# Second feed-forward network: the w3 product of all sixteen row tiles as seven block products, with the weight sums made in place

## The chip, the cores and the metric

One core of one Trainium2 chip runs one launch of the whole layer. The time is device microseconds of one execution. The engines that matter are the tensor engine (PE, with its weight loads as PEld), VectorE (DVE), ScalarE (ACT) and the queue of SyncE (SP), which issues the loads of weights. GpSimd (POOL) does next to nothing here.

## The reference

A layer with a gated feed-forward network before and after a mixer, in float32, for 256 rows of width 2048. The change touches only the second feed-forward network, cut here to what matters:

```python
h = _rms_norm(x, g_ffn2) * (1.0 + sc3) + sh3
x = x + 0.5 * ga3 * (jax.nn.silu(h @ w1_b) * (h @ w3_b)) @ w2_b      # w1_b, w3_b: 2048 x 5632, w2_b: 5632 x 2048
x = _rms_norm(x, g_final)
```

## The kernel before

**Precision.** Every float32 product is made of three passes: an operand is split into a high part (a cast to fp32r on ACT) and a low part (the value less the high part, on DVE), and `mm3` (lines 134 to 139) multiplies high by high, high by low and low by high. The activations `h`, transposed, are the stationary operand, the weights the moving one.

**Units and buffers.** Weights come in units of 4 row tiles of 128 by 512 columns (1 MB, one load, 128 x 2048). Three `raw` buffers receive them (pool `raws`, line 68). A unit is split in two halves of 128 x 1024; each half takes one of six `wh` and one of six `wl` buffers (pool `hl`, line 69). A half's buffer is used again six halves later, when PE has read it. So DVE and ACT run at most three units ahead of PE, and a raw buffer is loaded again when the splitting of the unit in it is done.

**Stages of the second network.** The 5632 columns are 11 chunks of 512, in groups: chunks 0 and 1, 2 to 4, 5 to 7, 8 to 10. For each group an up stretch makes `silu(h @ w1) * (h @ w3)`, and a down stretch (`ffn_down`) multiplies by `w2` and adds to `x`. In chunk 0 both up products are plain, 8 units of 24 matmuls of 512 columns. For chunks 1 to 10 the w1 product is plain (4 units, one per group of four row tiles, kg = 0 to 3). The w3 product is plain for kg = 3 and made of block products for kg = 0 to 2: a 2 x 2 by 2 x 2 block product (two row tiles, two halves of the rows of `h`, two blocks of 256 columns) by seven products in place of eight. `left_sums` makes the four sums of blocks of `h` once, in chunk 0 (their high and low parts are `sh`, `sl`). `seven_products` loads a unit whose blocks lie in the order (0,1), (0,0), (1,1), (1,0) for each of two q, makes four sums of weight blocks into a tile `T` of its own (lines 1242 to 1245), splits three raw blocks (768 columns) and four sums (1024 columns) for each q (lines 1252 and 1253), and runs 42 matmuls of 256 columns. They add up in the accumulator `a3` and two banks `m0`, `m1`, from which `sum_up` makes the w3 product at the end of the chunk.

**Order of the work.** The engines run their own queues in order. The program is written in the order of chunks; a scheduler places each engine's instructions by it and by its own times, keeping some matmuls in program order (`pin`). In a chunk the written order was: w1 unit 0, w3 unit 3, the transposes of the chunk before (`flush`), then three times seven products and a w1 unit, with `sum_up` ahead of the last unit.

## Time and profile before

| | |
|---|---|
| median of 3 runs | 2145.2 us (2145.12 to 2149.35) |
| profiled execution: its time, its span | 2147.01 us, 2145.2 us |
| PE busy, DVE busy, ACT busy | 99%, 76%, 48% of the span |
| granted tensor clock, mean | 0.995 |
| second feed-forward network | from about 1415 us on |

The span is the first to the last recorded instruction. Durations of DVE and ACT rows include the end of an instruction that the next one may overlap, and those of matmuls are modelled, so the prediction works with times from start to start.

### The profile page before, as it was taken

Reading aid. Unit: us, or ns where it says so; the run is one execution under the profiler, and the core shown is the slowest. Engines: PE = TensorE matmul, PEld = TensorE weight load, DVE = VectorE, ACT = ScalarE, POOL = GpSimd, SP = SyncE. Lnnn points to the kernel's source line nnn. Section 1 sums busy time; section 2 is a strip of 40 time slices with the busy share of each in tenths; the row PEclk is TensorE's granted clock in tenths of the full one; section 3 lists DMA queues with packets and bytes.
Section 4 is the critical chain, followed back from the end, with each engine's and each line's share of the span. In section 5 each row is a group of like instructions: output and inputs, shape, how many; then the busy total and the mean of one; then the engine's idle time right before and its main releaser. Section 6 shows DMA issues by size and latency. Waiting matters only on the chain.

```text
span 2145.2 us, 26028 instructions
## 1 busy us (share of the span) xinstructions
PE 2113.4 (99%) x10192; PEld 1759.2 (82%) x10192; DVE 1627.6 (76%) x1840; ACT 1036.7 (48%) x1290; POOL 41.7 (2%) x63
## 2 busy tenths in 40 slices
PE   8899999999999999999999999999999999999998
PEld 6677888888888879888877888878888888888886
DVE  6888767788778777565777788887788678857875
ACT  6434443334344465655544434475455445535553
POOL 0000000000000001010000000000000000000000
PEclk9999999999999999999999999999999999999999
DMA  9998768899899855445788788855555645655563
GB/s 368 347 361 322 246 222 322 329 351 346 335 327 334 323 174 188 167 172 199 287 286 306 285 328 312 339 209 188 206 194 189 208 176 196 215 196 195 178 216 118
DMA packets 78670, 550.30 MB, mean 257 GB/s; under 512 B 9361, under 2 KB 9921, under 8 KB 13266
## 3 DMA queue, kind: packets, MB, share of 16 engines
q1 hardware_dynamic: 75744, 542.06, 69.2%
q0 software_dynamic: 1344, 3.17, 0.5%
q10 hardware_dynamic: 1458, 3.40, 0.4%
q8 instruction: 80, 1.31, 0.2%
q14 instruction: 44, 0.36, 0.0%
HBM read 546.47 MB, written 2.12 MB: 256 GB/s over the span
## 4 chain that ended last, share of the span: by engine, by line
PE 90%; DVE 3%; DMA 3%; ACT 2%; issue 1%; POOL 0%; SPq 0%; POOLq 0%; ACTq 0%
PE a L135 9%; PE a L138 9%; PE a L139 9%; PE y L135 9%; PE y L139 9%; PE y L138 9%; DMA raw<-in_w_open 3%; PE pacc L138 2%; PE pacc L139 2%; PE pacc L135 2%; DVE wl L124 2%; PE qkv L135 1%; PE gb L135 1%; PE qkv L138 1%; PE ga L139 1%; PE ga L135 1%
## 5 line engine op out<-in xcount | busy, mean ns | idle before, releaser
L123 ACT CAST wh<-raw 128x1024 fp32r<-128x1024 f32 (+2 forms) x678 | 690.0, 1040 | 890.1 <-DMA raw<-in_w_a 212.9
L124 DVE TENSOR_TENSOR wl<-raw,wh 128x1024 fp32r<-128x1024 f32 (+2 forms) x678 | 804.3, 1208 | 337.1 <-ACT wh L123 335.2
L192 DVE SCALAR_TENSOR_TENSOR raw<-raw,c_bc 128x2048 f32<-128x2048 f32 x144 | 329.2, 2287 | 31.4 <-DMA raw<-in_w_ada 30.1
L135 PE MATMUL a<-wh,hTh 128*128 128x512 f32 (+1 forms) x904 | 340.1, 376 | 0.1
L138 PE MATMUL a<-wl,hTh 128*128 128x512 f32 (+1 forms) x904 | 339.4, 375 | 0.0
L139 PE MATMUL a<-wh,hTl 128*128 128x512 f32 (+1 forms) x904 | 339.2, 375 | 0.0
L135 PE MATMUL y<-wh,gT 128*128 128x512 f32 x704 | 275.7, 392 | 0.2
L138 PE MATMUL y<-wl,gT 128*128 128x512 f32 x704 | 274.1, 389 | 0.0
L139 PE MATMUL y<-wh,gT 128*128 128x512 f32 x704 | 273.7, 389 | 0.0
L139 PEld LDWEIGHTS a<-wh,hTl 128*128 128x128 f32 x904 | 170.2, 188 | 31.2 <-DVE hTl L363 0.3
L135 PEld LDWEIGHTS a<-wh,hTh 128*128 128x128 f32 x904 | 170.3, 188 | 30.3 <-ACT wh L123 0.6
L138 PEld LDWEIGHTS a<-wl,hTh 128*128 128x128 f32 x904 | 170.4, 188 | 29.1
L135 PEld LDWEIGHTS y<-wh,gT 128*128 128x128 f32 x704 | 132.2, 188 | 29.5 <-ACT gT L386 1.8
L139 PEld LDWEIGHTS y<-wh,gT 128*128 128x128 f32 x704 | 132.1, 188 | 27.7 <-DVE gT L387 0.2
L138 PEld LDWEIGHTS y<-wl,gT 128*128 128x128 f32 x704 | 132.2, 188 | 26.9
L138 PE MATMUL pacc<-wl,hTh 128*128 128x512 f32 x360 | 142.9, 397 | 6.7 <-DVE wl L124 6.7
L135 PE MATMUL pacc<-wh,hTh 128*128 128x512 f32 x360 | 138.4, 398 | 6.6 <-ACT wh L123 5.9
L139 PE MATMUL pacc<-wh,hTl 128*128 128x512 f32 x360 | 141.6, 393 | 0.7 <-DVE hTl L545 0.7
L1253 DVE TENSOR_TENSOR wl<-right,wh 128x1024 fp32r<-128x1024 f32 x60 | 73.4, 1224 | 30.6 <-ACT wh L1252 30.0
L1252 ACT CAST wh<-right 128x1024 fp32r<-128x1024 f32 x60 | 63.2, 1053 | 56.4 <-PE m L139 25.2
L138 PEld LDWEIGHTS pacc<-wl,hTh 128*128 128x128 f32 x360 | 68.4, 190 | 25.3 <-DVE wl L124 11.0
L135 PEld LDWEIGHTS pacc<-wh,hTh 128*128 128x128 f32 x360 | 67.8, 189 | 24.3 <-ACT wh L123 9.3
(350 smaller groups left out, 3096.1 us busy)
## 6 DMA issues: line engine op xcount, KB each, us to landing
raw<-in_w_ada SPq DMA_DIRECT2D x144, 1024.0 KB, 6.1
raw<-in_w_b SPq DMA_DIRECT2D x102, 1024.0 KB, 4.8
raw<-in_w_a SPq DMA_DIRECT2D x84, 1024.0 KB, 6.0
raw<-in_w_in SPq DMA_DIRECT2D x60, 1024.0 KB, 5.0
raw<-in_w_open SPq DMA_DIRECT2D x48, 1024.0 KB, 6.9
raw<-in_w_s SPq DMA_DIRECT2D x30, 1024.0 KB, 4.8
raw<-in_w_out SPq DMA_DIRECT2D x16, 1024.0 KB, 6.0
raw<-in_w_proj_a SPq DMA_DIRECT2D x8, 1024.0 KB, 4.8
```

The lines of the kernel that those rows point to most:

```text
L123: last_cast[0] = ACT.copy(wh[:, :w], src)
L124: DVE.tensor_tensor(wl[:, :w], src, wh[:, :w].bitcast(F32), op=ALU.subtract)
L135: m = PE.matmul(out, xh, wh, start=start, stop=False)
L138: PE.matmul(out, xh, wl, start=False, stop=False)
L139: PE.matmul(out, xl, wh, start=False, stop=stop)
L192: last_ada[0] = DVE.scalar_tensor_tensor(out=raw, in0=raw, scalar=1.0, in1=c_bc, op0=ALU.mult, op1=ALU.mult, accum_out=dst)
L1252: ACT.copy(wh[:, :n], src)
L1253: DVE.tensor_tensor(wl[:, :n], src, wh[:, :n].bitcast(F32), op=ALU.subtract)
```

## The change

`seven_products` runs for all four kg, so the plain w3 unit of chunks 1 to 10 goes and a fourth `left_sums` and a fourth unit of reordered weights come. The weight sums are no longer made into a tile of their own but in the raw buffer itself: the three raw blocks of both q are split first, then four sums of 128 x 2 x 256 overwrite the raw blocks, then the four sums of both q are split. The room of `T` goes to the fourth left tile; `left_sums` takes its work tile from the raw buffers. One corner of the accumulator is no longer written, so `sum_up` copies and adds 768 columns of it. In a chunk the written order is now: w1 unit 0, seven products kg = 0, `flush`, w1 unit 1, seven products 1, w1 unit 2, seven products 2, seven products 3, `sum_up`, w1 unit 3.

```diff
         def left_sums(kg):

-            t = f2.tile([P, D], F32, tag="T", name="left")
+            t = raws.tile([P, D], F32, tag="raw", name="left")
             f = t[:, :1024].rearrange("p (t k n) -> p t k n", t=TB, k=4)
             for tb in range(TB):
...
-            sh = f2.tile([P, 4, 2, P], F32R, name=f"sh{kg}")
-            sl = f2.tile([P, 4, 2, P], F32R, name=f"sl{kg}")
+            both = f2.tile([P, 2, 4, 2, P], F32R, tag=f"S{kg}", name=f"S{kg}")
             flat = lambda v: v.rearrange("p s q n -> p (s q n)")
-            ACT.copy(flat(sh), t[:, 1024:])
-            DVE.tensor_tensor(flat(sl), t[:, 1024:], flat(sh).bitcast(F32), op=ALU.subtract)
-            SH.append(sh)
-            SL.append(sl)
+            ACT.copy(flat(both[:, 0]), t[:, 1024:])
+            DVE.tensor_tensor(flat(both[:, 1]), t[:, 1024:], flat(both[:, 0]).bitcast(F32), op=ALU.subtract)
+            SH.append(both[:, 0])
+            SL.append(both[:, 1])

         def seven_products(acc, ms, ap, kg, first, last):
 
             raw = load_unit(ap)
             rv = raw.rearrange("p (q b n) -> p q b n", q=2, b=4)
-            t = f2.tile([P, D], F32, tag="T", name="right")
-            tv = t.rearrange("p (q b n) -> p q b n", q=2, b=4)
-            DVE.tensor_tensor(tv[:, :, 0:2], rv[:, :, 1:3], rv[:, :, 0:1].broadcast_to([P, 2, 2, 256]),
-                              op=ALU.subtract)
-            DVE.tensor_tensor(tv[:, :, 2], tv[:, :, 1], rv[:, :, 1], op=ALU.add)
-            DVE.tensor_tensor(tv[:, :, 3], rv[:, :, 3], tv[:, :, 2], op=ALU.subtract)
+            w = [[], []]
+
+            def split(q, b0, b1):
+                wh = hl.tile([P, 1024], F32R, tag="wh", name="wh")
+                wl = hl.tile([P, 1024], F32R, tag="wl", name="wl")
+                n = (b1 - b0) * 256
+                src = raw[:, q * 1024 + b0 * 256:q * 1024 + b1 * 256]
+                ACT.copy(wh[:, :n], src)
+                DVE.tensor_tensor(wl[:, :n], src, wh[:, :n].bitcast(F32), op=ALU.subtract)
+                w[q].extend((wh[:, i:i + 256], wl[:, i:i + 256]) for i in range(0, n, 256))
+
             for q in range(2):
-                w = []
-                for src in (raw[:, q * 1024 + 256:(q + 1) * 1024], t[:, q * 1024:(q + 1) * 1024]):
-                    n = src.shape[1]
-                    wh = hl.tile([P, 1024], F32R, tag="wh", name="wh")
-                    wl = hl.tile([P, 1024], F32R, tag="wl", name="wl")
-                    ACT.copy(wh[:, :n], src)
-                    DVE.tensor_tensor(wl[:, :n], src, wh[:, :n].bitcast(F32), op=ALU.subtract)
-                    w += [(wh[:, i:i + 256], wl[:, i:i + 256]) for i in range(0, n, 256)]
+                split(q, 1, 4)
+            DVE.tensor_tensor(rv[:, :, 2], rv[:, :, 2], rv[:, :, 0], op=ALU.subtract)
+            DVE.tensor_tensor(rv[:, :, 0], rv[:, :, 1], rv[:, :, 0], op=ALU.subtract)
+            DVE.tensor_tensor(rv[:, :, 1], rv[:, :, 1], rv[:, :, 2], op=ALU.add)
+            DVE.tensor_tensor(rv[:, :, 3], rv[:, :, 3], rv[:, :, 1], op=ALU.subtract)
+            for q in range(2):
+                split(q, 0, 4)
+            for q in range(2):
...
+                v = w[q]
                 for out, x, wt, is_first, is_last in (
-                        (ms[0][:, lo], xs(k, 0), w[0], True, False), (acc[:, 0, lo], xs(k + 1, 0), w[2], False, False),
-                        (acc[:, 0, hi], left(3), w[1], False, True), (ms[1][:, lo], left(0), w[3], True, False),
-                        (acc[:, 1, lo], xs(k + 1, 1), w[6], False, True), (ms[0][:, hi], left(1), w[5], False, True),
-                        (ms[1][:, hi], left(2), w[4], False, True)):
+                        (ms[0][:, lo], xs(k, 0), v[0], True, False), (acc[:, 0, lo], xs(k + 1, 0), v[2], True, False),
+                        (acc[:, 0, hi], left(3), v[1], False, True), (ms[1][:, lo], left(0), v[3], True, False),
+                        (acc[:, 1, lo], xs(k + 1, 1), v[6], True, True), (ms[0][:, hi], left(1), v[4], False, True),
+                        (ms[1][:, hi], left(2), v[5], False, True)):
                     mm3(out, *x, *wt, start=begin and is_first, stop=end and is_last, pin=begin or end)
...
             h = wkB("h3")
-            ACT.copy(h, acc.rearrange("p t n -> p (t n)"))
+            ACT.copy(h[:, :768], acc.rearrange("p t n -> p (t n)")[:, :768])
             r = wkA("r")
             u = r[:, 768:1024]
...
-            DVE.tensor_tensor(u, ms[1][:, 0:256], r[:, 512:768], op=ALU.add)
-            DVE.tensor_tensor(h, h, r, op=ALU.add)
+            DVE.tensor_tensor(h[:, 768:1024], ms[1][:, 0:256], r[:, 512:768], op=ALU.add)
+            DVE.tensor_tensor(h[:, :768], h[:, :768], r[:, :768], op=ALU.add)
...
-                    gemm(a3, up_units(a["w3_b"], c, xs), hook={kg: lambda kg=kg: left_sums(kg) for kg in range(3)})
+                    gemm(a3, up_units(a["w3_b"], c, xs), hook={kg: lambda kg=kg: left_sums(kg) for kg in range(4)})
...
                 a1 = acc_tile("a1")
                 unit(a1, a["w1_b"][0, c], 0, True, False)
                 a3 = acc_tile("a3")
                 ms = [bank("m0"), bank("m1")]
-                unit(a3, a["w3_b"][3, c], 3, True, False)
-                flush()
-                for kg in range(3):
-                    seven_products(a3, ms, a["w3_s"][kg, c - 1], kg, kg == 0, kg == 2)
-                    if kg == 2:
+                for kg in range(4):
+                    seven_products(a3, ms, a["w3_s"][kg, c - 1], kg, kg == 0, kg == 3)
+                    if kg == 3:
                         h3 = sum_up(a3, ms)
-                    unit(a1, a["w1_b"][kg + 1, c], kg + 1, False, kg == 2)
+                    if kg == 0:
+                        flush()
+                    if kg != 2:
+                        unit(a1, a["w1_b"][min(kg, 2) + 1, c], min(kg, 2) + 1, False, kg == 3)
...
-        gfin = f2.tile([P, D], F32, tag="T", name="gfin")
+        gfin = f2.tile([P, D], F32, tag="S0", name="gfin")
         ACT.dma_start(gfin, a["g_final"].to_broadcast([P, D]))
```

How this moves instructions, at three places. In the names, `wh` and `wl` are the high and low part of a half, `raw` a unit's buffer and `right` the tile of weight sums of before; the numbers tell tiles apart.

The first place is VectorE in chunk 2, from the end of the second seven products to the third. Before, where each q had its raw blocks and its sums split in turn, and the sums of the third stood beside the subtractions of the w1 unit ahead of it:

```order
L1253 TENSOR_TENSOR wl_11895<-raw_11859,wh_11894 128x768
L1253 TENSOR_TENSOR wl_11899<-right_11861,wh_11898 128x1024
L1242 TENSOR_TENSOR right_11959<-raw_11957 128x2x512
L1244 TENSOR_TENSOR right_11959<-right_11959,raw_11957 128x2x256
L124 TENSOR_TENSOR wl_11926<-raw_11923,wh_11925 128x1024
L1245 TENSOR_TENSOR right_11959<-raw_11957,right_11959 128x2x256
L124 TENSOR_TENSOR wl_11930<-raw_11923,wh_11929 128x1024
L1253 TENSOR_TENSOR wl_11964<-raw_11957,wh_11963 128x768
L1253 TENSOR_TENSOR wl_11968<-right_11959,wh_11967 128x1024
L1253 TENSOR_TENSOR wl_11993<-raw_11957,wh_11992 128x768
L1253 TENSOR_TENSOR wl_11997<-right_11959,wh_11996 128x1024
```

Now, from the third seven products (raw_11960) to the fourth (raw_12024):

```order
L1254 TENSOR_TENSOR raw_11960<-raw_11960 128x2x256
L1255 TENSOR_TENSOR raw_11960<-raw_11960 128x2x256
L1256 TENSOR_TENSOR raw_11960<-raw_11960 128x2x256
L1257 TENSOR_TENSOR raw_11960<-raw_11960 128x2x256
L1247 TENSOR_TENSOR wl_11975<-raw_11960,wh_11974 128x1024
L1247 TENSOR_TENSOR wl_11979<-raw_11960,wh_11978 128x1024
L1247 TENSOR_TENSOR wl_12027<-raw_12024,wh_12026 128x768
L1247 TENSOR_TENSOR wl_12031<-raw_12024,wh_12030 128x768
L1254 TENSOR_TENSOR raw_12024<-raw_12024 128x2x256
L1255 TENSOR_TENSOR raw_12024<-raw_12024 128x2x256
L1256 TENSOR_TENSOR raw_12024<-raw_12024 128x2x256
L1257 TENSOR_TENSOR raw_12024<-raw_12024 128x2x256
```

The four sums stand together between the splitting of the raw blocks and that of the sums, and no other work lies between them or behind them; the fourth seven products follow the third with no w1 unit between. ScalarE's casts at that place now stand so (L1246 is the cast in `split`):

```order
L1246 CAST wh_11962<-raw_11960 128x768
L1246 CAST wh_11966<-raw_11960 128x768
L1246 CAST wh_11974<-raw_11960 128x1024
L1246 CAST wh_11978<-raw_11960 128x1024
L1246 CAST wh_12026<-raw_12024 128x768
L1246 CAST wh_12030<-raw_12024 128x768
L1246 CAST wh_12038<-raw_12024 128x1024
L1246 CAST wh_12042<-raw_12024 128x1024
```

Before, ScalarE too alternated raw blocks and sums with two casts of a w1 unit between two seven products; now the casts of the sums come after both casts of raw blocks, and eight casts of seven products follow each other.

The second place is PE in the fourth seven products of chunk 2, from the last matmuls with the raw blocks of q = 0 (wh_12026) to those with its sums (wh_12038, wl_12039):

```order
L139 MATMUL a3_11761<-wh_12026,S3_10923 128x256
L135 MATMUL m1_11763<-wh_12038,S3_10923 128x256
L135 MATMUL a3_11761<-wh_12038,hTh_10579 128x256
L135 MATMUL m0_11762<-wh_12038,S3_10923 128x256
L138 MATMUL m1_11763<-wl_12039,S3_10923 128x256
L139 MATMUL m1_11763<-wh_12038,S3_10923 128x256
L138 MATMUL a3_11761<-wl_12039,hTh_10579 128x256
L139 MATMUL a3_11761<-wh_12038,hTl_10580 128x256
L138 MATMUL m0_11762<-wl_12039,S3_10923 128x256
L139 MATMUL m0_11762<-wh_12038,S3_10923 128x256
```

Three matmuls with the high part of the sums were moved ahead of the first with their low part.

The third place is VectorE where chunk 2 ends and chunk 3 begins: the tail of `sum_up`, the first seven products of chunk 3 (raw_12171) and the product with silu (L1324):

```order
L1247 TENSOR_TENSOR wl_12174<-raw_12171,wh_12173 128x768
L1247 TENSOR_TENSOR wl_12178<-raw_12171,wh_12177 128x768
L1254 TENSOR_TENSOR raw_12171<-raw_12171 128x2x256
L1324 TENSOR_TENSOR h3_12088<-h3_12088,silu_12130 128x1024
L1255 TENSOR_TENSOR raw_12171<-raw_12171 128x2x256
L1256 TENSOR_TENSOR raw_12171<-raw_12171 128x2x256
L1257 TENSOR_TENSOR raw_12171<-raw_12171 128x2x256
```

The product with silu, which waits for the end of chunk 2's last w1 unit, stands between the first and the second of the weight sums of chunk 3.

4 lines of the change are left out of this document (2 added, 2 removed).

## The prediction

> **What bounds the kernel now.** I read the page first: engine shares and the chain of work that ended last.
>
> ```profile
> span 2145.2 us, 26028 instructions
> PE 2113.4 (99%) x10192; PEld 1759.2 (82%) x10192; DVE 1627.6 (76%) x1840; ACT 1036.7 (48%) x1290; POOL 41.7 (2%) x63
> PE 90%; DVE 3%; DMA 3%; ACT 2%; issue 1%; POOL 0%; SPq 0%; POOLq 0%; ACTq 0%
> ```
>
> The tensor engine sets the end. But 76% for VectorE is a mean over the whole program; the change lies in the up stretches of the second FFN only, so I looked at one 512-column chunk there (c = 3), by its window, and at its ends in the chain.
>
> ```profile
> 1602.50:1645.75 43.25, 43.25 (x255) 38.47 (x254) 36.48 (x39) 24.75 (x27) 0.00 (x0) 1.00 0.55 195
> 1602.46 0.23 PE a L139
> 1645.72 0.23 PE a L139
> ```
>
> The columns of the first row are the wall time, then busy PE, PEld, DVE, ACT, POOL, then granted clock, DMA share and GB/s. PE is busy throughout at clock 1.00; one chunk takes 1645.72 - 1602.46 = 43.26 us. DVE is busy 36.48 us of it, so it has 6.8 us to spare per chunk. DMA is at 55%. The question is whether what the change takes from PE is worth more than what it puts on DVE's 6.8 us.
>
> **What it saves on PE.** Matmul durations overlap, so I take start-to-start times from PE's rows of chunk c = 2: seven products over one weight tile (42 matmuls of 256 columns), then one plain unit (24 of 512).
>
> ```profile
> 1549.26 0.39 PE L135 MATMUL a<-wh,hTh 128*128 128x512 f32 x1
> 1560.14 0.28 PE L135 MATMUL m<-wh,hTh 128*128 128x256 f32 x1
> 1562.54 0.28 PE L139 MATMUL m<-wh,sl 128*128 128x256 f32 x1
> 1565.17 0.40 PE L135 MATMUL a<-wh,hTh 128*128 128x512 f32 x1
> 1570.64 0.28 PE L135 MATMUL m<-wh,hTh 128*128 128x256 f32 x1
> 1591.64 0.39 PE L135 MATMUL a<-wh,hTh 128*128 128x512 f32 x1
> ```
>
> Seven products: 1565.17 - 1560.14 = 5.03 us, 0.120 per matmul. A unit: 1570.64 - 1565.17 = 5.47 us. Each of the ten chunks c = 1 to 10 swaps one unit for seven products: 0.44 us less, 4.4 us in all. That is the whole gain; 0.2% of the time is 4.3 us, about what a measurement of this kernel can tell from no change. One chunk of PE work becomes 43.26 - 0.44 = 42.82 us; the first of a group has no transposes: it takes 1591.64 - 1549.26 = 42.38 now and 41.94 after.
>
> **What it puts on DVE.** Here are DVE's rows around one block-sum sequence of before.
>
> ```profile
> 1544.11 0.69 DVE L1244 TENSOR_TENSOR right<-right,raw 128x512 f32<-128x512 f32 x1
> 1544.83 0.69 DVE L1245 TENSOR_TENSOR right<-raw,right 128x512 f32<-128x512 f32 x1
> 1592.68 0.95 DVE L1253 TENSOR_TENSOR wl<-raw,wh 128x768 fp32r<-128x768 f32 x1
> 1593.55 1.22 DVE L1316 TENSOR_TENSOR h<-h,silu 128x1024 f32<-128x1024 f32 x1
> 1594.68 0.69 DVE L1245 TENSOR_TENSOR right<-raw,right 128x512 f32<-128x512 f32 x1
> 1653.03 1.23 DVE L1253 TENSOR_TENSOR wl<-right,wh 128x1024 fp32r<-128x1024 f32 x1 [0.43 <-ACT wh L1252]
> 1654.29 1.23 DVE L1242 TENSOR_TENSOR right<-raw 128x1024 f32<-128x1024 f32 x1
> 1655.55 0.69 DVE L1244 TENSOR_TENSOR right<-right,raw 128x512 f32<-128x512 f32 x1
> 1656.16 1.22 DVE L124 TENSOR_TENSOR wl<-raw,wh 128x1024 fp32r<-128x1024 f32 x1
> ```
>
> Start to start, an independent follower comes after 1.14 us (1024 elements, 1593.55 to 1594.68), 0.87 (768, 1592.68 to 1593.55), 0.61 (512, 1655.55 to 1656.16). A follower that must wait for its predecessor comes later: 1.26 (L1253 to L1242, which overwrites what L1253 read), 0.72 (L1244 to L1245). In the changed kernel the four sums stand back to back, each overwrites or reads what the one ahead touched, and the first overwrites what the low-part subtraction ahead of it reads. So each pays the longer spacing. Before, other work stood between.
>
> The round trip to ScalarE comes on top. The casts of the sums can start only when the fourth sum is done, DVE's next instruction is their subtraction, and nothing stands between:
>
> ```profile
> 1561.41 0.84 ACT L1252 CAST wh<-raw 128x768 fp32r<-128x768 f32 x1
> 1562.90 1.05 ACT L1252 CAST wh<-right 128x1024 fp32r<-128x1024 f32 x1 [0.65 <-PE m L139]
> 1565.43 1.05 ACT L1252 CAST wh<-right 128x1024 fp32r<-128x1024 f32 x1 [0.60 <-PE m L139]
> 1566.52 1.22 DVE L1253 TENSOR_TENSOR wl<-right,wh 128x1024 fp32r<-128x1024 f32 x1 [0.44 <-ACT wh L1252]
> 1595.46 1.05 ACT L1252 CAST wh<-right 128x1024 fp32r<-128x1024 f32 x1 [2.59 <-DVE right L1245]
> ```
>
> DVE to ACT costs 0.09 (1594.68 + 0.69 to 1595.46), the cast 1.05, ACT to DVE 0.04 (1566.48 to 1566.52). Call the four halves of a tile p, q (raw blocks, 768) and r, s (sums, 1024). One seven on DVE is now: low part of p 0.87; of q 0.95 + 0.04 until the first sum; three sums at 0.72 and the last 0.69; the round trip 0.09 + 1.05 + 0.04 = 1.18; r and s 2 x 1.14 = 2.28. Sum: 8.17 us, against 5.03 us of matmuls.
>
> The rest of DVE's chunk:
>
> ```profile
> 1648.27 1.28 DVE L387 TENSOR_TENSOR gT<-gT_ps,gT 128x512 fp32r<-128x512 f32 x2
> 1673.73 0.42 DVE L1274 TENSOR_TENSOR r<-m,r 128x256 f32<-128x256 f32 x1
> 1674.25 0.69 DVE L1276 TENSOR_TENSOR r<-m,r 128x512 f32<-128x512 f32 x1
> 1674.86 1.22 DVE L124 TENSOR_TENSOR wl<-raw,wh 128x1024 fp32r<-128x1024 f32 x1
> ```
>
> Four units 4 x 2 x 1.14 = 9.12; the two gT parts 2 x 0.61 = 1.22; the block sums of the output 0.52 (1673.73 to 1674.25) + 0.72 + 0.34 + 0.87 = 2.45 (the 256 without a wait put at 0.34, an estimate from 0.42 less the 0.08 by which the longer ones overlap); the product with silu 1.14. With 4 x 8.17 = 32.68 this is 46.61 us per chunk, against PE's 42.82. DVE becomes the bound: a settled chunk goes from 43.26 to 46.6, plus 0.0 to 0.3 us where DVE waits for a buffer that PE has to free. I take 46.7: 3.4 us more.
>
> **Where PE will stand still.** Six split buffers let DVE and ACT run three units ahead. They hide a late tile when a plain unit follows (5.47 us of PE work for 2.28 us of DVE), but now the third and fourth sevens follow each other. Walk c = 2, the first of a group, from the start of its first unit W0, with the saturated PE: W0 0 to 5.46, S0 to 10.49, W1 to 15.95, S1 to 20.98, W2 to 26.44, S2 to 31.47. The cast of S2's q needs the buffer of S1's q, six halves earlier, which PE frees after S1's matmul 30, at 15.95 + 3.6 + 0.24 = 19.79 (0.24 is what passes from the end of a matmul's 0.12 slot to ACT's start: 1562.54 + 0.12 to 1562.90). Cast 0.84, low part at 20.67, sums from 21.66 to 24.5, cast of r to 25.65, low part of r at 25.69; then s 26.83, S3's p 27.97, q 28.84, its sums 29.83 to 32.68, cast to 33.82, low part of r done at 35.1. PE comes to S3 at 31.47 and can do p (nine matmuls) and, in the planned order, three with r's high parts: it needs the low part at 32.9. It waits 2.25 us. So a first chunk goes from 42.38 to 41.94 + 2.25 = 44.2: 1.8 us more.
>
> What waits behind: S3's end lets the output sums start, W3's end lets silu start, and DVE's product with silu stands in its queue ahead of the next S0's second sum, which is why later chunks settle at DVE's period and not at 44.2.
>
> **Left sums.** A fourth left_sums goes into chunk 0:
>
> ```profile
> 1437.20 1.29 DVE L1219 TENSOR_TENSOR left<-hTh,hTl 128x512 f32<-128x512 f32 x2
> 1438.40 1.23 DVE L124 TENSOR_TENSOR wl<-raw,wh 128x1024 fp32r<-128x1024 f32 x1
> 1439.54 0.42 DVE L1222 SCALAR_TENSOR_TENSOR left<-left 128x256 f32<-128x256 f32 x1
> 1439.87 0.42 DVE L1226 TENSOR_TENSOR left<-left 128x256 f32<-128x256 f32 x1
> raw<-in_w_b SPq DMA_DIRECT2D x102, 1024.0 KB, 4.8
> ```
>
> It costs DVE 1.2 + 4 x 0.34 + 1.14 = 3.7 us. All four now take a turn in the three raw buffers, so the load of w3's third unit starts only when the second left sum has been split, and lands 4.8 us later. By my walk that unit comes 1 to 1.5 us late to PE. Bounds: 0, hidden by the three units ahead, and 8.5, all of 3.7 and a whole landing. I take 1.0, near the lower bound, since PE has 5.47 us per unit and three are ready. The tile for g_final takes S0's place, free before the last down stretch: 0, hidden by that stretch; uncovered, its landing.
>
> **The sum.** Settled chunks 3, 4, 6, 7, 9, 10: 6 x 3.4 = 20.4. First chunks 2, 5, 8: 3 x 1.8 = 5.4. Chunk 1, which begins after chunk 0 but carries gT parts: 3.4, like a settled one. Left sums 1.0. Together 30.2 us. The profiled execution had a span of 2145.2 and took 2147.0, within 0.1% of the median of 2145.2; from the median I get 2175.4, say 2175.
>
> One rule of the Trainium skill speaks for less. VectorE: DVE Perf Modes, section "The DRAIN you can't avoid", reports eight copies that took 13.88 us with a semaphore after each and with one after the last alone, so that a wait on the predecessor costs nothing extra. This trace does not agree: 1.26 against 1.14 and 0.72 against 0.61. By that rule the sum would be the first rival's.
>
> **The rivals.** (1) The waits between the sums cost nothing: 0.87 for q, 0.61 for three sums, so a seven takes 8.17 - 0.12 - 0.33 = 7.72 us and a settled chunk 46.7 - 1.8 = 44.9. Then 6 x 1.6 + 3 x 0.9 (S2 and S3 each save 0.45) + 1.6 + 1.0 = 14.9: 2160. For it: the forms of L1242 and L1244 only resemble the new ones. Against it: both rows above show the longer spacing.
>
> (2) The other side: PE stays the bound. DVE's debt is carried by the six buffers through the chunks and paid back in the down stretches, where DVE has nothing but 2.28 us per 5.47 us unit. The place is S3; it decides where a seven costs DVE no more than (42.82 - 13.93) / 4 = 7.2 us (13.93 is the chunk's other work), that is where about 1 us of the round trip is filled. Then the 4.4 us are gained: 2141. For it: 6.8 us of spare time in DVE's window. Against it: DVE's queue is in order and holds no other work behind the fourth sum.
>
> (3) The raw ring binds: left sums and tiles held longer make loads late, 8.5 us instead of 1.0 in chunk 0: 2183. For it: the in-place tile is freed only after s. Against it: a tile's next load has two other units (over 10 us) before it is wanted, against 4.8.
>
> **How the numbers follow.** Forecast 0.62, rival 1 0.18, rival 2 0.09, rival 3 0.11. Rival 2 in full is faster by about 0.2%, so I split it: faster 0.07, same 0.04 with half-covered cases; slower 0.89. The forecast's own range is 2166 to 2184: 0.2 us per seven either way, 8 us over forty. For 8 in 10 the range reaches below rival 1 and above rival 3: 2153 to 2187; rival 2 stays out.
>
> **What would show it.** Right: chunk-to-chunk distance of 46 to 47 us; DVE busy over 90% in such a window; PE waiting in the fourth seven for wl, over 2 us each; the four sums 0.72 apart; DVE's idle time before r's low part about 1.1 us, named ACT wh. Wrong: a distance of 42.8 and no PE wait (rival 2), sums 0.61 apart and 45 us (rival 1), PE or ACT waiting on DMA for raw (rival 3).

## The result and the profile after

| | before | after |
|---|---|---|
| median of 4 runs each | 2146.9 us (2145.1 to 2149.4) | 2179.7 us (2176.2 to 2184.2) |
| ratio after / before | | 1.0158, 95% interval 1.0140 to 1.0176 |
| profiled execution: time, span | 2147.0, 2145.2 us | 2177.5, 2175.7 us |
| settled chunk (c = 3, 4, 6, 7, 9, 10) | 43.25 to 43.26 us | 47.5 to 48.0 us |

The change makes the kernel 32.7 us slower. The page of after, span, engine shares and chain of waits:

```profile
span 2175.7 us, 26495 instructions
PE 2127.4 (98%) x10372; PEld 1778.1 (82%) x10372; DVE 1677.2 (77%) x1937; ACT 1037.3 (48%) x1311; POOL 41.6 (2%) x63
PE 76%; DVE 15%; ACT 4%; DMA 3%; issue 2%; POOL 0%; SPq 0%; ACTq 0%; POOLq 0%; DVEq 0%
```

The shares of busy time hardly move; the chain does. VectorE's part of it goes from 3% to 15%, 12% of the span, and TensorE's from 90% to 76%. A busy share says how much an engine works, the chain who is waited for.

Where the time went shows in stretches cut at the start of silu (line 1315 before, 1323 after), one silu per chunk. Of after, the first chunk of a group with the down stretch ahead of it (c = 2), then the two settled chunks c = 3 and 4, by windows (wall time, busy PE, PEld, DVE, ACT, POOL, granted clock, DMA share, GB/s):

```profile
1505.70:1594.00 88.30, 87.60 (x468) 75.11 (x467) 68.86 (x71) 41.89 (x49) 3.26 (x6) 1.00 0.56 195
1594.00:1641.75 47.75, 45.33 (x273) 40.75 (x272) 42.24 (x49) 24.73 (x30) 0.00 (x0) 0.96 0.50 186
1641.75:1689.78 48.03, 45.32 (x273) 40.78 (x272) 41.03 (x46) 25.14 (x29) 0.00 (x0) 0.96 0.49 167
```

The first two of the same stretches of before (the third takes 43.25):

```profile
1504.19:1591.84 87.65, 87.65 (x451) 74.59 (x450) 65.28 (x63) 42.06 (x47) 4.41 (x8) 1.00 0.58 204
1591.84:1635.10 43.26, 43.26 (x255) 38.47 (x254) 36.48 (x39) 24.75 (x27) 0.00 (x0) 1.00 0.56 195
```

Over the program: the six settled chunks 26.7 us longer together (4.45 each); the first chunks of the three groups 0.65, 0.85 and 0.77, together 2.3; chunks 0 and 1, from the transposes that feed chunk 0 to the silu of chunk 1, 91.15 in place of 85.69, so 5.5; after the last silu 76.04 in place of 76.07. That is 34.4 us. In this execution everything ahead of chunk 0 happened to end 3.95 us earlier (those transposes start at 1414.55 in place of 1418.50), so the spans differ by 30.5. This opening moves by that much between executions of the same code, as a run below with the same opening shows, and is no part of the change.

VectorE's rows in c = 3 of after, from r's low part of the third seven to the next chunk's product with silu:

```profile
1621.43 4.10 DVE L1247 TENSOR_TENSOR wl<-raw,wh 128x1024 fp32r<-128x1024 f32 x4 [1.17 <-ACT wh L1246]
1625.57 0.69 DVE L1254 TENSOR_TENSOR raw<-raw 128x512 f32<-128x512 f32 x1
1626.29 0.69 DVE L1255 TENSOR_TENSOR raw<-raw 128x512 f32<-128x512 f32 x1
1627.02 0.69 DVE L1256 TENSOR_TENSOR raw<-raw 128x512 f32<-128x512 f32 x1
1627.74 0.69 DVE L1257 TENSOR_TENSOR raw<-raw 128x512 f32<-128x512 f32 x1
1629.62 2.36 DVE L1247 TENSOR_TENSOR wl<-raw,wh 128x1024 fp32r<-128x1024 f32 x2 [1.19 <-ACT wh L1246]
...
1642.81 1.22 DVE L1324 TENSOR_TENSOR h<-h,silu 128x1024 f32<-128x1024 f32 x1 [1.13 <-ACT silu L1323]
```

From r's low part to r's low part of the next seven it is 1629.62 - 1621.43 = 8.19 us, with no other work between. The sums start 0.72 to 0.73 apart, and VectorE stands idle for 1.17 to 1.19 us until ScalarE has cast the sums. The wait in the last row is new in this chunk: VectorE also stands idle for 1.13 us until silu is done. The reason stands in PE's rows of the same seven, the fourth:

```profile
1627.60 0.28 PE L139 MATMUL a<-wh,S 128*128 128x256 f32 x1
1629.64 0.39 PE L135 MATMUL m<-wh,S 128*128 128x256 f32 x1 [1.76 <-ACT wh L1246]
...
1629.98 0.28 PE L135 MATMUL m<-wh,S 128*128 128x256 f32 x1
1630.90 0.39 PE L138 MATMUL m<-wl,S 128*128 128x256 f32 x1 [0.64 <-DVE wl L1247]
...
1634.20 0.41 PE L138 MATMUL a<-wl,S 128*128 128x256 f32 x1
1634.41 0.41 PE L139 MATMUL a<-wh,S 128*128 128x256 f32 x1
```

After p's nine products PE loses 1.92 us to the cast of r (2.04 from start to start, less 0.12 for the product), and 0.80 us to r's low part. From then on the products start 0.21 us apart and not 0.12. The granted clock (the column behind the busy times) in windows of 2 us says why:

```profile
1629.00:1631.00 2.00, 0.72 (x4) 0.52 (x4) 1.38 (x2) 2.00 (x3) 0.00 (x0) 1.00 0.00 0
1631.00:1633.00 2.00, 2.00 (x11) 2.00 (x12) 2.00 (x2) 2.00 (x3) 0.00 (x0) 0.57 0.11 16
1633.00:1635.00 2.00, 2.00 (x12) 2.00 (x12) 2.00 (x3) 1.33 (x2) 0.00 (x0) 0.58 0.78 274
1635.00:1637.00 2.00, 2.00 (x15) 1.84 (x14) 1.85 (x3) 1.29 (x3) 0.00 (x0) 1.00 1.03 434
```

Behind the stall the tensor clock falls to 0.57 for about 3.5 us. Seventeen products at 0.21 in place of 0.12 are about 1.5 us, and these put back the last w1 unit, silu, and VectorE's product with silu, which stands in its queue ahead of the next sums. The clock falls so in all seven chunks that have this stall (c = 1, 3, 4, 6, 7, 9, 10), and in no first chunk of a group.

### The profile page after: what moved, and what is told of

Read it like the earlier page. It is cut to its first block, busy times and chain, and to the rows that moved or that the text cites. A ratio compares the mean times of both kernels' runs of the same rounds, so it can differ in the third digit from the quotient of the medians.

```text
span 2175.7 us, 26495 instructions
## 1 busy us (share of the span) xinstructions
PE 2127.4 (98%) x10372; PEld 1778.1 (82%) x10372; DVE 1677.2 (77%) x1937; ACT 1037.3 (48%) x1311; POOL 41.6 (2%) x63
## 4 chain that ended last, share of the span: by engine, by line
PE 76%; DVE 15%; ACT 4%; DMA 3%; issue 2%; POOL 0%; SPq 0%; ACTq 0%; POOLq 0%; DVEq 0%
PE y L135 8%; PE y L139 8%; PE y L138 8%; PE a L139 5%; PE a L138 5%; PE a L135 5%; DVE wl L1247 5%; DVE wl L124 4%; PE pacc L138 2%; PE pacc L139 2%; PE pacc L135 2%; DMA raw<-in_w_open 2%; ACT wh L1246 2%; PE qkv L135 1%; PE gb L135 1%
## 5 line engine op out<-in xcount | busy, mean ns | idle before, releaser
L123 ACT CAST wh<-raw 128x1024 fp32r<-128x1024 f32 (+2 forms) x658 | 663.5, 1039 | 770.8 <-DMA raw<-in_w_a 223.7
L124 DVE TENSOR_TENSOR wl<-raw,wh 128x1024 fp32r<-128x1024 f32 (+2 forms) x658 | 776.9, 1207 | 295.5 <-ACT wh L123 292.9
L135 PE MATMUL a<-wh,hTh 128*128 128x512 f32 (+1 forms) x864 | 321.6, 372 | 0.1
L138 PE MATMUL a<-wl,hTh 128*128 128x512 f32 (+1 forms) x864 | 321.2, 372 | 0.0
L139 PE MATMUL a<-wh,hTl 128*128 128x512 f32 (+1 forms) x864 | 320.8, 371 | 0.0
L1246 ACT CAST wh<-raw 128x768 fp32r<-128x768 f32 (+1 forms) x160 | 142.9, 940 | 195.9 <-DVE raw L1257 159.7
L1247 DVE TENSOR_TENSOR wl<-raw,wh 128x768 fp32r<-128x768 f32 (+1 forms) x160 | 167.4, 1087 | 52.7 <-ACT wh L1246 52.5
L139 PEld LDWEIGHTS a<-wh,hTl 128*128 128x128 f32 x864 | 164.4, 190 | 27.8 <-DVE hTl L363 0.3
L138 PEld LDWEIGHTS a<-wl,hTh 128*128 128x128 f32 x864 | 164.7, 191 | 26.4 <-DVE wl L124 0.2
L135 PEld LDWEIGHTS a<-wh,hTh 128*128 128x128 f32 x864 | 163.9, 190 | 27.2 <-ACT wh L123 0.6
```

Of the source, the lines that this page charges most:

```text
L123: last_cast[0] = ACT.copy(wh[:, :w], src)
L124: DVE.tensor_tensor(wl[:, :w], src, wh[:, :w].bitcast(F32), op=ALU.subtract)
L135: m = PE.matmul(out, xh, wh, start=start, stop=False)
L138: PE.matmul(out, xh, wl, start=False, stop=False)
L139: PE.matmul(out, xl, wh, start=False, stop=stop)
L1246: ACT.copy(wh[:, :n], src)
```

## The experiments

The theory: VectorE's rows in order, four sevens of 8.2 us and 14 us of other work, set the settled chunk (46.6 us), and the fallen clock adds the last 1.1 us through silu. Rivals: in-place sums are slow wherever they stand; the two sevens in a row stall PE whatever a seven costs; the clock costs nothing; the left sums have a share. Medians, ratios to the kernel before as measured beside each run, and two settled chunks of the profiled execution, from silu to silu:

| run | median us | ratio, 95% interval | c = 3, c = 4, us |
|---|---|---|---|
| e1 sums in place alone | 2145.6 | 0.9998, 0.9986 to 1.0009 | 43.26, 43.25 |
| e2 units between all sevens | 2155.2 | 1.0036, 1.0023 to 1.0049 | 43.33, 45.34 |
| e3 clock kept busy, 16 products | 2168.9 | 1.0102, 1.0083 to 1.0121 | 46.54, 47.57 |
| e4 same unit in the round trip | 2199.6 | 1.0246, 1.0227 to 1.0265 | 53.16, 50.91 |
| e5 sums ahead in work tiles | 2140.9 | 0.9979, 0.9969 to 0.9990 | 42.85, 42.86 |
| e6 those sums on GpSimd | 2175.9 | 1.0149, 1.0133 to 1.0164 | 47.31, 48.02 |
| e7 next unit in the round trip | 2147.6 | 1.0010, 1.0001 to 1.0019 | 43.34, 43.34 |
| e8 left sums in the raw ring | 2148.0 | 1.0009, 0.9996 to 1.0022 | 43.26, 43.26 |
| e9 e5 plus one row | 2163.1 | 1.0081, 1.0061 to 1.0101 | 44.98, 44.58 |
| e10 e5 plus two rows | 2209.4 | 1.0289, 1.0270 to 1.0308 | 51.76, 49.28 |
| e11 clock, 8 products | 2172.6 | 1.0122, 1.0097 to 1.0146 | 47.99, 48.00 |

**e1: the sums in place, nothing else of the change.** `seven_products` of before gets the body of after (casts of p and q, four sums in the raw buffer, casts of r and s); three sevens, the old order.

```diff
-            t = f2.tile([P, D], F32, tag="T", name="right")
-            tv = t.rearrange("p (q b n) -> p q b n", q=2, b=4)
-            DVE.tensor_tensor(tv[:, :, 0:2], rv[:, :, 1:3], rv[:, :, 0:1].broadcast_to([P, 2, 2, 256]),
-                              op=ALU.subtract)
...
+            for q in range(2):
+                split(q, 1, 4)
+            DVE.tensor_tensor(rv[:, :, 2], rv[:, :, 2], rv[:, :, 0], op=ALU.subtract)
...
+            for q in range(2):
+                split(q, 0, 4)
```

> The kernel before with one part of the change: the weight sums of its three sevens are made in place in the raw buffer, with the casts before and after; the row tiles of kg 3 stay a plain w3 unit, and the order of the units is the old one. Computes the whole reference. Theory (the change loses because DVE's chunk of four in-place sevens, 46.6 us, is longer than PE's 42.8; the in-place seven is harmless while DVE has room): three sevens at 8.17 + five units at 2.28 + 4.8 for gT, sum_up and the silu product = 40.7 us of DVE against a measured 43.26 us per settled chunk. The chunk stays at 43.2 to 43.5 and the time at 2145 to 2150. Rival (a seven in place costs its longer start wherever it stands, since PE waits for each low part of r): about 0.5 to 1.2 us for each of 30 sevens, 2160 to 2180. A clock that falls would need a stall of about 3 us on PE, which neither expects here.

No change to within the measurement, and 43.26 us a chunk as before. Its VectorE pays the same price: four sums 0.72 apart and a wait before r's low part,

```profile
1637.01 0.69 DVE L1258 TENSOR_TENSOR raw<-raw 128x512 f32<-128x512 f32 x1
1638.91 2.36 DVE L1248 TENSOR_TENSOR wl<-raw,wh 128x1024 fp32r<-128x1024 f32 x2 [1.20 <-ACT wh L1247]
```

but PE never waits (busy 43.26 of 43.26). So in-place sums are not slow as such; a longer seven costs nothing as long as VectorE has room. Its opening, the same code as before's, ended 3.4 us earlier (first of the last transposes at 1415.07 against 1418.50), while the medians agree: that is the variation left out above.

**e2: the same rows, no two sevens in a row.**

```diff
                 for kg in range(4):
+                    if kg:
+                        unit(a1, a["w1_b"][kg, c], kg, False, kg == 3)
                     seven_products(a3, ms, a["w3_s"][kg, c - 1], kg, kg == 0, kg == 3)
-                    if kg == 3:
-                        h3 = sum_up(a3, ms)
...
-                    if kg != 2:
-                        unit(a1, a["w1_b"][min(kg, 2) + 1, c], min(kg, 2) + 1, False, kg == 3)
+                h3 = sum_up(a3, ms)
```

> The changed kernel with the last w1 unit moved between the third and the fourth seven (order w1 unit, seven, four times over; the sums at the end), so that no two sevens are neighbours. Computes the whole reference. Theory (DVE's sum of work sets the chunk): DVE's rows are the same 46.6 us, so a settled chunk is 46 to 47 us; the stall of 2 us at the fourth seven is spread or gone, so the clock stays at 1.00 and the wait of DVE for silu (1.1 us) goes. Six settled chunks at -1.1 us: 2170 to 2175, still 25 us above before. Rival (the loss is the stall of two sevens in a row and nothing else): the chunk falls to PE's 42.8 to 43.3 us and the time to 2143 to 2150.

Between the two: 2155, and neither expectation holds for every chunk. c = 3 takes 43.33, c = 4 takes 45.34, and so in all three groups (43.34 and 45.32; 43.31 and 45.29). VectorE's rows at the border of c = 3 and 4, and r's low parts of the second and the third seven of c = 4:

```profile
1633.21 0.68 DVE L1254 TENSOR_TENSOR raw<-raw 128x512 f32<-128x512 f32 x1
1633.81 0.68 DVE L1283 TENSOR_TENSOR r<-m,r 128x512 f32<-128x512 f32 x1
1634.41 0.68 DVE L1255 TENSOR_TENSOR raw<-raw 128x512 f32<-128x512 f32 x1
...
1651.38 2.36 DVE L1247 TENSOR_TENSOR wl<-raw,wh 128x1024 fp32r<-128x1024 f32 x2 [1.17 <-ACT wh L1246]
...
1661.84 2.36 DVE L1247 TENSOR_TENSOR wl<-raw,wh 128x1024 fp32r<-128x1024 f32 x2 [1.17 <-ACT wh L1246]
```

Two things are read here. Where `sum_up`'s rows fall between the sums, these start 0.60 after their neighbour and not 0.72, so the waits are filled there; VectorE's period becomes 45.7 us (r of the second seven at 1605.70 in c = 3 and 1651.38 in c = 4) and not 46.6. And a unit with its seven takes VectorE 1661.84 - 1651.38 = 10.46 us, PE 5.47 + 5.03 = 10.50: evenly matched. VectorE falls behind only at the chunk's border, by 2 to 3 us, and the six buffers carry that once, through c = 3; c = 4 pays. In the changed order the third and fourth sevens make VectorE lose 16.4 - 10.1 = 6.3 us in one place in every chunk, more than the buffers hold. So "the chunk is VectorE's sum" is a limit that a group of three chunks need not reach, and the order decides how much of it is paid: 2179.7 - 2155.2 = 24.5 us of the loss hang on it, the fallen clock's share among them.

**e3: the clock.**

```diff
+                    if extra and q == 0 and wt is v[3]:
+                        for _ in range(extra):
+                            tc.keep_in_program_order(PE.matmul(acc[:, 1, hi], xs(k, 0)[0], v[0][0], start=False, stop=False))
-                    mm3(out, *x, *wt, start=begin and is_first, stop=end and is_last, pin=begin or end)
+                    mm3(out, *x, *wt, start=begin and is_first, stop=end and is_last, pin=begin or end or (extra and q == 0))
...
-                    seven_products(a3, ms, a["w3_s"][kg, c - 1], kg, kg == 0, kg == 3)
+                    seven_products(a3, ms, a["w3_s"][kg, c - 1], kg, kg == 0, kg == 3,
+                                   16 if kg == 3 and c not in (2, 5, 8) else 0)
```

> The changed kernel with 16 further 256-wide products (1.9 us) put on PE in the fourth seven ahead of r's products, into a corner of the sums that nobody reads, in chunks 1, 3, 4, 6, 7, 9 and 10. Computes the whole reference. Theory (the last 1.1 us of a settled chunk's +4.45 comes from a tensor clock of 0.57 for 3.5 us after PE stood still for 2.0 and 0.9 us): PE has work during the stall, the clock stays at 1.00, silu is 1.5 us earlier, DVE's product no longer waits for it, and a settled chunk falls from 47.7 to 46.6; 7 chunks make -7 to -8 us, about 2172. Rival (the clock is a by-product and costs nothing, the chunk is what DVE's rows add up to): no change within 1 us, 2178 to 2181. Third case: the products end after the wait would have and delay PE by up to 1 us a chunk: 2180 to 2187.

2168.9, 10.7 us less than the changed kernel and 3 less than expected. Of the profiled executions' 10.7, 1.5 is the opening; 9.2 lie in the chunks, counted to PE's last w1 product: 1.0 in chunk 1, 1.0 to 1.5 in each of five settled chunks, 2.2 in c = 10. Giving PE more work made the kernel faster. In c = 3 the added products end before the wait does, and the clock stays:

```profile
1625.28 2.08 PE L1274 MATMUL a<-wh,hTh 128*128 128x256 f32 x16
1627.19 0.39 PE L135 MATMUL m<-wh,S 128*128 128x256 f32 x1
1628.45 0.39 PE L138 MATMUL m<-wl,S 128*128 128x256 f32 x1 [0.87 <-DVE wl L1247]
1628.67 0.28 PE L139 MATMUL m<-wh,S 128*128 128x256 f32 x1
1628.79 0.28 PE L135 MATMUL a<-wh,hTh 128*128 128x256 f32 x1
```

The products behind the stall start 0.12 apart, no stretch of slow products occurs in any chunk, and c = 3 takes 46.54, c = 6 46.53, c = 9 46.52: the 46.6 of the prediction. From silu to silu the second settled chunks (47.57, 46.85, 46.70) look longer. That is the mark and not the work: in c = 4 PE starts its last w1 product at 1684.13, 46.50 us after that of c = 3, but ScalarE has silu in its queue behind a cast of the down stretch, which waits for its load:

```profile
1684.68 1.05 ACT L123 CAST wh<-raw 128x1024 fp32r<-128x1024 f32 x1 [0.75 <-DMA raw<-in_w_b]
1685.63 1.02 ACT L1327 ACTIVATE silu<-a 128x1024 f32<-128x1024 f32 x1
```

Counted to PE's last w1 product the second settled chunks take 46.50, 46.50 and, in c = 10, where PE hardly waits for r, 45.43. The edit also keeps the products of q = 0 in program order; e11, below, has that too, and there chunks with and without the fall stand side by side.

**e4 and e7: filling the round trip.** Both use e2's order and put half a w1 unit's low part between the fourth sum and r's low part: e4 the second half of the unit that PE takes just before this seven, e7 the first half of the next unit.

Of e4:

```diff
+            half(0)
             for q in range(2):
                 split(q, 1, 4)
...
-            DVE.tensor_tensor(rv[:, :, 3], rv[:, :, 3], rv[:, :, 1], op=ALU.subtract)
+            fourth = [DVE.tensor_tensor(rv[:, :, 3], rv[:, :, 3], rv[:, :, 1], op=ALU.subtract)]
+            half(1)
             for q in range(2):
                 split(q, 0, 4)
```

Of e7, where `mid` casts the next unit's first half and its second half follows the seven:

```diff
-            DVE.tensor_tensor(rv[:, :, 3], rv[:, :, 3], rv[:, :, 1], op=ALU.subtract)
+            fourth = DVE.tensor_tensor(rv[:, :, 3], rv[:, :, 3], rv[:, :, 1], op=ALU.subtract)
+            if mid:
+                mid(fourth)
             for q in range(2):
                 split(q, 0, 4)
```

> The changed kernel in the order of the run with w1 units between all sevens, and with DVE given other work in the 1.2 us in which it waits for ACT's cast of r: the low part of the second half of the w1 unit stands between the fourth sum and r's low part, that of the first half ahead of q. Computes the whole reference. Theory (of 8.17 us a seven, 1.18 are DVE waiting for a cast that ACT can only begin after the fourth sum): the wait is filled with 1.14 us of work that stands elsewhere otherwise, so DVE's chunk falls by 4 x 1.18 = 4.7 us from 46.6 to 41.9, below PE's 42.8. PE then sets the chunk: 42.8 to 43.4, time 2141 to 2150. Rival (the waits between dependent sums and not the round trip are what counts, or the units come too late for PE): the chunk stays at 45 us or more, 2165 or more.

> The changed kernel in the order w1 unit, seven, four times over; the low part of the next unit's first half (not the same unit's second half, which PE waits for) stands between the fourth sum and r's low part. Computes the whole reference. Theory: in the run with units between all sevens DVE's period is 45.7 us, with three round trips of 1.17 idle a chunk; 1.14 us of work that stands elsewhere otherwise moves into each, so the period falls to 42.2 to 42.5, under PE's 42.8. PE sets the chunk at 42.8 to 43.3: 10 chunks at 0 to -0.44 against before, 2141 to 2147. Rival (the sums themselves, or the late r, hold PE up as before): chunks of 45 every second time, 2152 to 2158.

e4 missed by 50 us; of its rival, the part that the units come too late for PE came true. In it PE's unit waits for its own second half, which now stands behind four sums:

```profile
1605.00 0.79 PE L138 MATMUL a<-wl,hTh 128*128 128x512 f32 x1 [4.00 <-DVE wl L1247]
```

Cheap work for VectorE was put ahead of what PE wanted next; it tells nothing of the round trip. e7 does: in its c = 4 the filled wait

```profile
1650.92 0.69 DVE L1257 TENSOR_TENSOR raw<-raw 128x512 f32<-128x512 f32 x1
1651.53 1.22 DVE L1305 TENSOR_TENSOR wl<-raw,wh 128x1024 fp32r<-128x1024 f32 x1
1652.81 2.36 DVE L1247 TENSOR_TENSOR wl<-raw,wh 128x1024 fp32r<-128x1024 f32 x2
```

has no idle time, and every settled chunk takes 43.34 to 43.42: the second ones lose the 2 us that e2 had. PE sets the chunk, as expected, with 0.5 us over its 42.8; 0.33 of it are lost at the border, where the next chunk's first unit follows the fourth seven at once and waits:

```profile
1635.69 0.28 PE L139 MATMUL m<-wh,S 128*128 128x256 f32 x1
1636.14 0.50 PE L135 MATMUL a<-wh,hTh 128*128 128x512 f32 x1 [0.17 <-ACT h L1279]
```

So the median, 2147.6, lies just above the expected 2141 to 2147, and the 4.4 us that PE saves are not seen in it.

**e5: the sums ahead of the casts.** Three sums for each q go into a work tile; then come the casts and low parts of p and r for q = 0, and the same for q = 1.

```diff
+            for q in range(2):
+                t = (wkA if q == 0 else wkB)("right")
+                tv = t.rearrange("p (b n) -> p b n", b=4)
+                DVE.tensor_tensor(tv[:, 0:2], rv[:, q, 1:3], rv[:, q, 0:1].broadcast_to([P, 2, 256]), op=ALU.subtract)
+                DVE.tensor_tensor(tv[:, 2], tv[:, 1], rv[:, q, 1], op=ALU.add)
+                DVE.tensor_tensor(tv[:, 3], rv[:, q, 3], tv[:, 2], op=ALU.subtract)
...
+            for q in range(2):
+                for src in (raw[:, q * 1024 + 256:(q + 1) * 1024], ts[q]):
```

> The changed kernel in its own order of units, but the weight sums go into two work tiles of 1024 columns (one for each q) instead of the raw buffer and are made ahead of the casts, three instructions for each q; r's and s's casts no longer wait behind sums that wait behind p's and q's casts. Computes the whole reference. Theory (the length of DVE's seven decides, threshold 7.2 us): low parts 0.87 + 0.99 + 2 x 1.14, and for each q 1.3 to 1.6 of sums, 6.7 to 7.3 in all; DVE's chunk is 40.7 to 43.1, about PE's 42.8. The settled chunk is 42.8 to 43.8 and the time 2142 to 2152, with no stall of 2 us and a clock of 1.00. Rival (the neighbouring third and fourth seven stall PE whatever a seven costs): 45 us or more, above 2165.

It is faster than both kernels, and 1 us faster than expected: ratio to before 0.9979 (0.9969 to 0.9990), and 42.85 us in every settled chunk, PE busy throughout, with the third and fourth seven still in a row:

```profile
1587.44:1630.29 42.85, 42.85 (x273) 39.05 (x272) 40.57 (x55) 25.77 (x29) 0.00 (x0) 1.00 0.59 197
```

The sums of one q now stand between low parts of the other, and nearly no wait is left:

```profile
1608.74 1.22 DVE L1254 TENSOR_TENSOR wl<-right,wh 128x1024 fp32r<-128x1024 f32 x1
1609.88 0.42 DVE L1247 TENSOR_TENSOR right<-raw,right 128x256 f32<-128x256 f32 x1
1610.21 0.95 DVE L1254 TENSOR_TENSOR wl<-raw,wh 128x768 fp32r<-128x768 f32 x1
1611.08 0.69 DVE L1245 TENSOR_TENSOR right<-raw 128x512 f32<-128x512 f32 x1
1611.68 1.22 DVE L1254 TENSOR_TENSOR wl<-right,wh 128x1024 fp32r<-128x1024 f32 x1
```

A seven is 2 x (0.87 + 1.14 + 0.60 + 0.34 + 0.34) = 6.6 us. So the seven products for kg = 3 do gain what PE saves; what lost it was where the sums stood in VectorE's order, since with them ahead a seven costs VectorE 6.6 us and not 8.2. It also fells the rival that two sevens in a row stall PE whatever they cost.

**e9 and e10: e5 made longer.** One (e9, shown) or two (e10, without the condition) further rows of 1024 columns a seven, and nothing else.

```diff
                 tv = t.rearrange("p (b n) -> p b n", b=4)
+                if q == 0:
+                    DVE.tensor_tensor(t, raw[:, q * 1024:(q + 1) * 1024], raw[:, q * 1024:(q + 1) * 1024], op=ALU.add)
```

> The run with the sums ahead in work tiles, and one further DVE row of 1024 columns (1.14 us) for each seven, written into a work tile ahead of the sums that overwrite it: DVE gets longer, and nothing else changes. Computes the whole reference. DVE's rows in that run add up to about 40 us a chunk (4 sevens at 6.6, 4 units at 2.28, 4.5 of others), PE's to 42.85. Theory (the sum of DVE's rows against PE's 42.85 decides, carried over by the buffers): 40 + 4 x 1.14 = 44.5; the first settled chunk of a group may still be carried (42.9 to 44.5), the second is 44 to 45; 2146 to 2155. Rival (only the dependent start of a seven matters, which this row leaves as it is apart from 1.14 us): 42.85 throughout, 2140 to 2143.

> As the run before it with two such rows for each seven, 2.28 us. Computes the whole reference. Theory: DVE's chunk is 40 + 9.1 = 49 us, and every settled chunk 48.5 to 50 (a fall of the clock after long stalls changes nothing where DVE is the bound, except by up to 1 us through the wait for silu); 2185 to 2200. Rival: 42.85 to 44, below 2155.

The second settled chunks of the groups take 44.58, 44.58 and 44.55 in e9 (44.5 expected) and 49.28, 50.20 and 49.23 in e10 (49): 42.85 as long as PE is longer, then VectorE's sum. The first settled chunks took 44.98, 44.00 and 43.99 in e9 and 51.76, 50.73 and 51.94 in e10, where at most 50 had been expected. VectorE is busy there too (51.37 us of 51.76 in c = 3), with 67 rows against 62 in c = 4; why more of its rows fall there was not settled. In e10's c = 4 VectorE is busy 48.44 us of 49.28, and the clock falls again:

```profile
1657.22:1706.50 49.28, 45.31 (x273) 40.74 (x272) 48.44 (x62) 26.96 (x32) 0.00 (x0) 0.97 0.49 170
```

Both medians lie 8 to 9 us above the upper end of what was expected. In e9 the groups' first chunks took 2.1 to 3.8 us more than in e5, which the expectation had left at nothing, and chunk 1 1.5 us more; PE stands in c = 2 for 1.2 and 0.9 us in the first seven, whose added rows come behind the residual sums that end the down stretch (they start at 1550.11 and 1552.38). The 3.8 us are c = 8, where the clock fell behind this stall, at a cost of 1.5 us.

**e6: the sums on GpSimd.** e5 with `POOL.tensor_tensor` for the six sums.

> As the run with the sums ahead in work tiles, with the six sums of each seven on GpSimd, which stands idle in this stage. Computes the whole reference. Theory (DVE sets the chunk and is relieved): DVE's seven falls to 4.1 us, its chunk to 30; PE sets 42.8 if GpSimd makes its six sums in under 10 us, time 2141 to 2146. Rival (GpSimd becomes the bound; no row of this trace has its price for such a sum): four sevens at more than 10.7 us, above 2150 and without an upper limit that the trace gives. A second rival: GpSimd's sums slow DVE's rows while both run; then DVE's rows are longer than 1.14 us for a low part of 1024.

No gain: 2175.9. The groups of VectorE and then GpSimd over c = 3 and 4:

```profile
L124 DVE TENSOR_TENSOR wl<-raw,wh 128x1024 fp32r<-128x1024 f32 x18 | 25.5, 1462 | 0.4 <-ACT wh L123 0.4
```

```profile
L1245 POOL TENSOR_TENSOR right<-raw 128x512 f32<-128x512 f32 x15 | 27.9, 1869 | 18.1 <-DMA raw<-in_w_s 13.4 <-DVE h L1282 2.4 <-DVE wl L1254 2.3
```

The second rival is seen: a low part of 1024 has a mean of 1462 ns against 1220 in e5. Of the 34 such rows, the 14 with no sum on GpSimd beside them took 1.21 to 1.23 us; 12 of the other 20 took 1.75 to 2.31. A sum of 512 takes GpSimd 1869 ns in the mean against VectorE's 686. But GpSimd is not the bound that the first rival meant: its six sums take 2 x (1.87 + 1.46 + 0.99) = 8.6 us, under the 10 us of the theory, and in c = 3 it is busy for 33.8 us of 47.31, VectorE for 38.9. What makes the chunk longer, as far as the rows show it, is waiting in turn: GpSimd waits for the weights to land (13.4 us in two chunks), ScalarE for GpSimd's last sum (3.8 to 5.8 us in each seven of c = 3), and PE then for r (0.88 us before its low part in c = 3). How these add up to 47.3 was not worked out. The Trainium skill (SBUF — State Buffer, section "SBUF: two separate sides") says that these two engines share one pair of ports, held by one instruction at a time; the stretched rows agree with it.

**e8: the left sums in the raw ring, alone**, on top of e1.

```diff
-            t = f2.tile([P, D], F32, tag="T", name="left")
+            t = raws.tile([P, D], F32, tag="raw", name="left")
```

> The kernel before with in-place weight sums and, in addition, the left sums' temporary taken from the ring of raw buffers, in chunk 0 alone. Computes the whole reference. The prediction gave this 1.0 us with bounds of 0 to 8.5. Theory after reading the changed kernel's trace (no idle time of PE in chunk 0): 0 to 0.5 us, 2145 to 2148. Rival (the late loads that ACT's casts wait for, 3.4 and 3.0 us, reach PE): 3 to 6 us, 2149 to 2153.

Its median is 1.3 us above before's, with an interval of -0.9 to 4.7 us that holds nothing as well; the profiled stretch from the transposes to chunk 1's silu is 86.02 against 85.69, so 0.3 us, and in e5, which has all four left sums there and 0.44 us less for PE in chunk 1, 85.42. The 3 to 6 us of the rival are excluded in these profiles; 0.3 is what is left.

**e11: where the clock falls.** e3 with 8 products.

> The changed kernel with 8 further products (0.96 us) in the fourth seven in place of the 16 of the earlier run. Computes the whole reference. In the changed kernel PE stands still for 1.8 to 2.0 us, runs for 0.6, stands for 0.64, and the clock falls to 0.57; with 16 products the one stall left is 0.87 us and the clock stays. Here a stall of about 0.9 to 1.1 us and another of 0.64 to 0.87 are expected within 2.5 us. If the clock answers to the sum of idle time in some window, it still falls, or for a shorter time (silu distance 47 to 47.7, about 2176); if it answers to one long stall, it stays at 1.00 (46.5, about 2169).

Both happened (two runs, one profile). The same two stalls stand in each of six chunks; here c = 3 and c = 6:

```profile
1628.80 0.38 PE L135 MATMUL m<-wh,S 128*128 128x256 f32 x1 [0.80 <-ACT wh L1246]
1630.06 0.39 PE L138 MATMUL m<-wl,S 128*128 128x256 f32 x1 [0.88 <-DVE wl L1247]
```

```profile
1834.52 0.39 PE L135 MATMUL m<-wh,S 128*128 128x256 f32 x1 [0.79 <-ACT wh L1246]
1835.78 0.39 PE L138 MATMUL m<-wl,S 128*128 128x256 f32 x1 [0.87 <-DVE wl L1247]
```

Behind the first the clock falls and the chunk takes 47.99; behind the second it stays at 1.00 and the chunk takes 46.51. It fell in five chunks of the seven; in c = 10 only the second of the two stalls is recorded, and it stayed. The 1.5 us between 47.99 and 46.51, with everything else alike, is the price of one fall. It also shows that no stall of about 3 us is needed for a fall, as e1's expectation had it.

## Why the prediction was right, and which terms were off

2175 was forecast, 2179.7 measured, inside its range; the likeliest case, VectorE as the bound, was the right one. That the sum came so close is in part luck, since terms were wrong in both directions.

- **A seven on VectorE, 8.17 us:** 8.19 measured. The sums 0.72 apart, the round trip of 1.17 to 1.19 named ACT wh: as worked out from rows of other operations of before. Rival 1, that the waits cost nothing, falls with them.
- **VectorE becomes the bound:** shown by e9 and e10 against e5, where only VectorE's rows differ, by e5, where a shorter seven gives the chunk back to PE, and by e1, where the same seven costs nothing because VectorE has 40.7 us to do. The threshold of 7.2 us a seven lies between e5 (6.6, PE-bound) and e9 (7.7, 44.6 us).
- **A settled chunk 3.4 us longer:** 4.45. The term was mis-sized by the clock, which the prediction held at 1.00. The walk ended PE's last unit 1.5 us too early, and so saw no wait for silu; e3 takes the fall away and finds 46.5, e11 shows 46.5 and 48.0 side by side. Six chunks make 6.3 us of the miss.
- **The signs:** the sums' spacing and the wait named ACT wh came as said; three did not. The distance is 47.5 to 48.0 and not 46 to 47, by the clock. VectorE's busy share in c = 3 is 42.24 / 47.75 = 88% and not over 90, and the clock is not why, since e3 has 41.27 / 46.54 = 89%: the prediction's own sum holds four round trips of 1.18 us, a tenth of the chunk. And PE's wait is not one of over 2 us for wl but 1.92 us for r's cast and 0.80 for its low part. The walk's own times say so: PE is done with p at 31.47 + 9 x 0.12 = 32.55, r's cast only at 33.82, so no product with r's high part could run before.
- **A first chunk 1.8 us longer:** 0.65 to 0.85. The step that failed is "The cast of S2's q needs the buffer of S1's q". ScalarE's rows of the casts of p and q in c = 2 of after:

```profile
1567.85 0.83 ACT L1246 CAST wh<-raw 128x768 fp32r<-128x768 f32 x1
1569.25 0.84 ACT L1246 CAST wh<-raw 128x768 fp32r<-128x768 f32 x1 [0.56 <-PE m L139]
```

  The second seven starts on PE at 1566.54. With 0.24 us from slot to cast, what freed the buffer ended at 1569.01, 2.5 us in: that is matmul 21, the last with r, and not matmul 30, the last with q, at 3.6. So by this row q took the buffer that PE freed next, r's, which comes free before q's, and not the one of six halves earlier. The walk was 1.1 us late, and the wait of 2.25 us is 1.02 (0.22 and 0.80). The clock did not fall after it.
- **Chunk 1 and the left sums, 3.4 + 1.0:** 5.5 together. The left sums have at most some 0.3 of it (e8, e5); the rest is chunk 1, which has the stall and the fall of the clock of a settled chunk, and a wait of 0.69 us for r's low part in its first seven. Rival 3 is out, though its sign was half there: in chunk 0 ScalarE's casts wait 3.42 and 3.04 us for raw loads, which they do not before, but PE does not wait for them.
- **Rival 2, the debt carried by the buffers:** wrong for this order, but it is what happens in e2's first settled chunks. The prediction took 46.6 as a law of VectorE's rows; it is one only where the order makes VectorE lose more in one place than six buffers hold.

The errors partly cancelled, which is luck: 6.3 and 1.1 us too little for the settled chunks and chunk 1, 3.1 too much for the first chunks. The sum of the terms was 30.2, the traces give 34.4.

Left open: how the waits of e6 add up to its chunk; why the first settled chunks of e10 hold more of VectorE's rows; and what a tile for the sums beside the raw buffer with the old tile kept would cost, since with the fourth left tile there is no room for it.

## What to carry to other kernels

Before moving work onto an engine "with spare time", add up its rows of one loop pass start to start, with the waits between dependent neighbours and each round trip to another engine, and compare with the bound's pass: a mean of 76% told nothing here, 46.6 against 42.8 did. Independent work between dependent instructions is worth more than fewer instructions: e5 has more rows than the changed kernel, with the sums ahead of the casts, and takes 39 us less. A stall of PE costs more than its length when the clock falls behind it, so count PE's idle time near to it, too.
